# Block 7's rows of v summed by TensorE per token, alternating with block 6's rows summed by VectorE

## The chip, the cores and the metric

The kernel runs on one core of a Trainium2 chip. The metric is the device time of one execution in microseconds (us), as the median over runs. Engines are named as the profile names them: PE is TensorE (PEld its weight loads), DVE is VectorE, ACT is ScalarE, POOL is GpSimd, SP is SyncE. All compute engines work through their instructions in a fixed order that was set when the program was built.

## The reference

One layer over 1024 tokens of width 1024: a mixing part (RWKV-7 and latent attention, gated and added to x), then PEER, then a per-layer embedding and a last RMSNorm. The change lies in PEER, a retrieval over 16384 single-neuron experts. For each token 8 heads choose 16 experts each by product keys, so 128 expert numbers `idx` and 128 gates per token:

```python
act = jax.nn.gelu(jnp.einsum('td,thkd->thk', xb, u_tab[idx]), approximate=False)
return jnp.einsum('thk,thkd->td', gate * act, v_tab[idx])
```

`xb` is the normed x of a block of 128 tokens; `u_tab` and `v_tab` are tables of 16384 rows of 1024 f32 numbers. What is added to x is, for each token, a sum of 128 rows of `v_tab`, each times its own weight. After PEER comes `x + sigmoid(RMSNorm(x) @ W_pg) * (p @ W_ple)` and the final norm.

## The kernel before, in words

The 1024 tokens are eight blocks of 128, in four slices of two blocks for the mixing part. `everything` (L1064) lists the stages with a priority each; a scheduler builds from it the fixed order of each engine's instructions: of those that it takes to be ready, the smaller number goes first. So stages interleave. A tile in a pool has a tag and a number of buffers; a new tile of the same tag waits until the oldest buffer's last reader is done.

The weights of a block's experts are made by `gather` (L891): for each k of 128, POOL issues an indirect DMA (L900) that brings to partition t the row of u that token t has chosen as its k-th, and DVE multiplies it with h and sums it up (L902). After gelu the result goes into `gate`, 128 tokens by 128 choices.

The rows of v are summed in two ways. Blocks 0 to 4 go through `dense` (L968, priority 50): `expand` has written for each of them a matrix of weights, mostly zeros, over all 16384 experts, and `dense` multiplies it with the whole table v, read once. Of each piece of v (`vr`, 128x512) ACT makes a rounded part `vhi` (L280) and DVE the rest `vlo` (L282); PE then does three matmuls for each of the five blocks (L996 to L998), and after each eight pieces DVE adds the five accumulators to x (L1001). The five accumulators fill five banks of PSUM.

Blocks 5, 6 and 7 go through `add_rows` (L908, priorities 56, 57 and 58). For each k POOL gathers into a buffer, for all 128 tokens at once, the k-th row of v (L915, 512 KB), and DVE does x = x + row * gate[:, k] (L917). x of blocks 5 and 6 lies in the pool `xp`; x of block 7 takes the buffer `gh`, in which `gather` had its h, so the profile calls it gh. `row` (L882) hands out the buffers of the rows: a ring of seven (three tags of 3, 1 and 3 buffers), used by `gather` and `add_rows` alike. A gather into a buffer can be issued when the row that was in it has been used.

Last comes `ple` (L1019, priority 60) for the blocks in turn: `begin` squares and norms x, transposes it by PE in eight steps, with ACT and DVE splitting each into two parts; `end` does 60 matmuls, adds and norms, and writes the block out. It starts the `begin` of the next block before the `end` of a block. It can begin a block when that block's sum is complete.

Of the kernel before, what the change touches and what calls it, by code (L numbers as in the profile page):

```python
# [8 lines left out]
F = mybir.dt.float32  # L9
R = mybir.dt.float32r  # L10
I32 = mybir.dt.int32
# [3 lines left out]
OP = mybir.AluOpType  # L15
# [5 lines left out]
D = 1024  # L21
# [130 lines left out]
class Program:  # L152
# [752 lines left out]
            nc.vector.tensor_tensor(gate, gate, dots, op=OP.mult)  # L905


    def add_rows(self, b):  # L908
        nc = self.nc
        idx, gate = self.idx[b], self.gate[b]  # L910
        x = self.tile(*((self.gp, [128, D], F, "gh", 1) if b == 7 else (self.xp, [128, D], F, f"x{b}", 1)))
        nc.sync.dma_start(x, self.x1[b])
        for k in range(128):
            v = self.row()
            nc.gpsimd.indirect_dma_start(out=v[:], out_offset=None, in_=self.I["v"],  # L915
                                         in_offset=bass.IndirectOffsetOnAxis(ap=idx[:, k:k + 1], axis=0))
            nc.vector.scalar_tensor_tensor(x, v, gate[:, k:k + 1], x, op0=OP.mult, op1=OP.add)  # L917
        self.final[b] = x


    def expand(self, blocks, side="right"):
# [142 lines left out]
    def everything(self):  # L1064
        nc = self.nc
        order = [
            (0, self.project_rwkv, 0), (0.1, self.rwkv, 0), (0.2, self.project_rest, 0), (1, self.attend, 0),
            (1.5, self.select, 0), (50, self.gather, [0, 1]), (2, self.project_rwkv, 1), 
            (4.9, self.rwkv, 1), (5, self.project_rest, 1), (5.2, self.project_rwkv, 2), (5.5, self.attend, 1), (6, self.select, 1),
            (50, self.gather, [2, 3]),  # L1070
            (11.1, self.rwkv, 2), (10, self.project_rest, 2), 
            (11.2, self.project_rwkv, 3), (10.5, self.attend, 2), (11, self.select, 2), (51, self.gather, [4]),
            (49, self.expand, [0]), (16.1, self.rwkv, 3), (15, self.project_rest, 3), (49.5, self.attend, 3), (52.5, self.select, 3),
            (52, self.gather, [5]), (49, self.expand, [1, 2, 3, 4]), (60, self.ple_weights, 0), (53, self.more_rows, None),
            (53, self.gather, [6, 7]), (50, self.dense, 0),
            (56, self.add_rows, 5), (57, self.add_rows, 6), (58, self.add_rows, 7),
            (59, self.ple_weights, 1), (60, self.ple, range(8)),
        ]
        with ExitStack() as st:
            self.kp = self.pool(self.ctx, "cx", "right")  # L1080
            self.wp = self.pool(st, "wts", "left")
            begun = {}
            self.tc.cur_priority = PHASE // 20
            self.rope_tables()
            for prio, f, a in order:
                if f == self.more_rows:
                    st.close()
                    self.xp = self.pool(self.ctx, "dx", "left")
                    self.gp2 = self.pool(self.ctx, "rows", "left")
                    continue  # L1090
                self.tc.cur_priority = int(prio * PHASE)
                self.aux = nc.gpsimd if f == self.rwkv else nc.vector
                if f == self.project_rwkv:
                    begun[a] = f(a)
                elif f == self.attend:
                    f(a)
                    if a + 1 in begun:
                        begun[a + 1][1].close()
                elif f == self.project_rest:
                    begun[a][1].close()  # L1100
                    f(a, begun[a])
                elif f == self.ple_weights:
                    f(a, ("right", "left")[a])
                else:
                    f(a)
# [15 lines left out]
```

## Time and profile before

| | us |
|---|---|
| runs | 3947.78, 3949.66, 3959.03 |
| median of the runs | 3949.66 |
| the profiled execution's own time | 3942.72 |
| its span, first to last instruction | 3940.7 |
| PE busy | 3087.6 (78%) |
| DVE busy | 3193.8 (81%) |
| ACT busy | 1276.9 (32%) |
| POOL busy | 2050.4 (52%) |

The page gives each engine's busy time over the whole span. The stages differ, so the shares over the span say little about one of them; the views by stretch, further down, do that. Matmuls overlap in the engine, so PE's mean time of one matmul is longer than the distance from one to the next.

### The profile page before, as it was taken

What the parts mean: (1) busy time and instruction counts of PE and PEld (TensorE: products, weight loads), DVE (VectorE), ACT (ScalarE), POOL (GpSimd) and SP (SyncE); (2) the same over time, 40 slices, a digit from 0 to 9 for tenths busy, and PEclk for the clock granted to TensorE, in tenths of its full rate; (3) what the DMA queues carried; (4) which work ended last, traced back from release to release, by engine and by line L of the source; (5) the groups of instructions that cost most, each with busy time, mean ns of one, the idle gap of its engine ahead of it and who ended that gap; (6) DMA issues with size and microseconds to landing.
All of it is one profiled execution on the core that took longest, in us unless ns stands there. A gap on an engine that the chain in (4) does not pass through costs nothing.

```text
span 3940.7 us, 62191 instructions
## 1 busy us (share of the span) xinstructions
PE 3087.6 (78%) x21999; PEld 2517.8 (64%) x21999; DVE 3193.8 (81%) x6931; ACT 1276.9 (32%) x2723; POOL 2050.4 (52%) x1638
## 2 busy tenths in 40 slices
PE   7998778678879794878866687568888889989581
PEld 7885767666668673578735567446666667767351
DVE  2532888767899685899878778998999999999997
ACT  3231222133222174222138867522221222222341
POOL 0201456645654533576454425446767776666754
PEclk9998899888989796888967788779999999999796
DMA  6236598899868998878888998799999999999986
GB/s 200 88 112 200 183 321 286 285 318 309 313 188 309 322 323 285 305 243 279 311 276 284 302 336 274 233 321 341 386 384 371 390 379 372 373 385 352 329 279 232
DMA packets 502327, 1160.48 MB, mean 294 GB/s; under 512 B 54016, under 2 KB 228352, under 8 KB 502016
## 3 DMA queue, kind: packets, MB, share of 16 engines
q0 software_dynamic: 202752, 738.29, 52.7%
q1 hardware_dynamic: 281984, 402.48, 30.3%
q10 hardware_dynamic: 17280, 15.74, 1.2%
q8 instruction: 174, 2.85, 0.3%
q14 instruction: 137, 1.12, 0.1%
HBM read 1071.38 MB, written 84.93 MB: 293 GB/s over the span
## 4 chain that ended last, share of the span: by engine, by line
DVE 23%; PE 23%; issue 20%; DMA 17%; POOL 10%; ACT 5%; SPq 2%; POOLq 0%; DVEq 0%; ACTq 0%
DVE u L902 9%; DMA u<-in_u_dram,idx 9%; PE mm L290 7%; POOL u L900 6%; POOL u L915 4%; PE mm L785 2%; DVE oa L959 2%; PE w L961 1%; PE inv L586 1%; PE acc L997 1%; DMA u<-in_v_dram,idx 1%; DMA raw<-zT 1%; PE acc L998 1%; PE mm L292 1%; SPq L964 1%
## 5 line engine op out<-in xcount | busy, mean ns | idle before, releaser
L900 POOL DMA_INDIRECT u<-in_u_dram,idx x1024 | 1230.5, 1202 | 1182.1 <-DVE dots L902 625.2
L902 DVE CUSTOM_DVE_ANT_0 u<-u,gh 128x1024 f32<-128x1024 f32 x1024 | 1320.8, 1303 | 226.8 <-DMA u<-in_u_dram,idx 210.1
L915 POOL DMA_INDIRECT u<-in_v_dram,idx x384 | 485.7, 1265 | 230.6 <-DVE x L917 104.1
L290 PE MATMUL mm<-hT,w 128*128 128x128 f32 x4608 | 568.4, 284 | 11.8 <-DMA raw<-zT 3.5
L997 PE MATMUL acc<-vlo,Whi 128*128 128x512 f32 x1280 | 521.8, 408 | 67.4 <-DVE vlo L282 66.8
L290 PEld LDWEIGHTS mm<-hT,w 128*128 128x128 f32 x4608 | 553.1, 199 | 27.6 <-ACT z L326 7.8
L998 PE MATMUL acc<-vhi,Wlo 128*128 128x512 f32 x1280 | 513.4, 401 | 0.0
L996 PE MATMUL acc<-vhi,Whi 128*128 128x512 f32 x1280 | 374.3, 402 | 101.8 <-ACT vhi L280 83.0
L996 PEld LDWEIGHTS acc<-vhi,Whi 128*128 128x128 f32 x1280 | 244.9, 193 | 176.5 <-ACT vhi L280 93.1
L997 PEld LDWEIGHTS acc<-vlo,Whi 128*128 128x128 f32 x1280 | 248.4, 194 | 147.1 <-DVE vlo L282 96.7
L917 DVE SCALAR_TENSOR_TENSOR x<-u,gate,x 128x1024 f32<-128x1024 f32 x256 | 329.2, 1286 | 6.0 <-DMA u<-in_v_dram,idx 2.1
L280 ACT ACTIVATE vhi<-vr 128x512 fp32r<-128x512 f32 x256 | 158.8, 628 | 532.2 <-DMA vr<-in_v_dram 347.6
L961 PE MATMUL w<-ob,oa 128*128 128x128 f32 x1280 | 225.3, 334 | 98.1 <-ACT ob L955 53.5
L961 PEld LDWEIGHTS w<-ob,oa 128*128 128x128 f32 x1280 | 203.6, 240 | 124.9 <-ACT ob L955 81.6
L998 PEld LDWEIGHTS acc<-vhi,Wlo 128*128 128x128 f32 x1280 | 249.1, 195 | 51.6
L959 DVE TENSOR_SCALAR oa<-cst,pt 128x128 f32<-128x128 f32 x640 | 210.7, 388 | 39.3 <-PE w L961 34.8
L954 ACT ACTIVATE ob<-cst,pt 128x128 f32<-128x128 f32 x640 | 204.3, 396 | 0.6 <-PE w L961 0.5
L282 DVE TENSOR_TENSOR vlo<-vr,vhi 128x512 fp32r<-128x512 f32 x256 | 174.7, 693 | 8.0 <-ACT vhi L280 7.9
L280 ACT ACTIVATE Whi<-wr 128x1280 fp32r<-128x1280 f32 x64 | 81.5, 1273 | 287.0 <-PE acc L997 257.6
L917 DVE SCALAR_TENSOR_TENSOR gh<-u,gate,gh 128x1024 f32<-128x1024 f32 x128 | 167.9, 1311 | 4.9 <-DMA u<-in_v_dram,idx 3.0
L290 PE MATMUL mm<-act,w 128*128 128x256 f32 x512 | 134.0, 417 | 45.2 <-DMA act<-yg 29.1
L621 POOL TENSOR_TENSOR lm<-gs,cst 128x256 f32<-128x256 f32 x96 | 100.1, 1063 | 100.9 <-DVE gs L612 56.6
(331 smaller groups left out, 5511.6 us busy)
## 6 DMA issues: line engine op xcount, KB each, us to landing
w<-in_w_in_dram SPq DMA_DIRECT2D x144, 512.0 KB
vr<-in_v_dram SPq DMA_DIRECT2D x256, 256.0 KB
W<-ws SPq DMA_DIRECT2D x40, 1024.0 KB
wr<-W SPq DMA_DIRECT2D x64, 640.0 KB
w<-in_w_q_dram SPq DMA_DIRECT2D x64, 512.0 KB
w<-in_w_out_dram SPq DMA_DIRECT2D x32, 512.0 KB
u<-in_u_dram,idx POOLq DMA_INDIRECT x1024, 6.9
x<-in_x_dram SPq DMA_DIRECT2D x16, 512.0 KB
```

The lines of the kernel that those rows point to most:

```text
L280: self.nc.scalar.activation(act[0], x, AF.Copy)
L290: mm(ps, w[0][:, i], a[0][:, i], start=first, stop=last)
L900: nc.gpsimd.indirect_dma_start(out=u[:], out_offset=None, in_=self.I["u"], in_offset=bass.IndirectOffsetOnAxis(ap=idx[:, k:k + 1], axis=0))
L902: nc.vector.tensor_tensor_reduce(out=u[:], in0=u[:], in1=h[:], scale=1.0, scalar=0.0, op0=OP.mult, op1=OP.add, accum_out=dots[:, k:k + 1])
L915: nc.gpsimd.indirect_dma_start(out=v[:], out_offset=None, in_=self.I["v"], in_offset=bass.IndirectOffsetOnAxis(ap=idx[:, k:k + 1], axis=0))
L917: nc.vector.scalar_tensor_tensor(x, v, gate[:, k:k + 1], x, op0=OP.mult, op1=OP.add)
L954: nc.scalar.activation(c[:, i], self.c("iota"), AF.Abs, bias=pt[:, 1, k + i:k + i + 1])
L959: nc.vector.tensor_scalar(a, self.c("iota"), pt[:, 0, k:k + 1], pt[:, 2, k:k + 1], op0=OP.is_equal, op1=OP.mult)
L961: nc.tensor.matmul(ps[:, i], a, c[:, i], start=True, stop=True)
L996: nc.tensor.matmul(acc[b], wh, vh, start=i == 0, stop=False)
L997: nc.tensor.matmul(acc[b], wh, vl, start=False, stop=False)
L998: nc.tensor.matmul(acc[b], wl, vh, start=False, stop=i == G - 1)
```

## The change

`add_rows` takes a list of blocks. Block 5 is summed as before. Blocks 6 and 7 are one call, at priority 57: after every four rows of block 6, one step of the generator `sum_rows` runs for block 7. It gathers per token instead of per choice: `idx` and `gate` are transposed by PE, so that one gather brings to the 128 partitions the 128 chosen rows of one token. A matmul with weights of 128 rows by 32 columns, of which only the token's own column is not zero (it holds the token's 128 gates), adds the token's sum to its own row of PSUM and zeros to 31 others. Four tokens, 32j + i for j = 0 to 3, have their 32 columns side by side and write to the four quarters of the same two banks (one for each half of the 1024 columns); over the 32 steps i all 128 tokens are summed. DVE prepares the weights for four steps at a time, and at the end adds the two banks to x.

```diff
--- before.py
+++ after.py
@@ -905,17 +905,67 @@
             nc.vector.tensor_tensor(gate, gate, dots, op=OP.mult)
 
 
-    def add_rows(self, b):
-        nc = self.nc
-        idx, gate = self.idx[b], self.gate[b]
+    def rows_of_v(self, idx, k):
+        v = self.row()
+        self.nc.gpsimd.indirect_dma_start(out=v[:], out_offset=None, in_=self.I["v"],
+                                          in_offset=bass.IndirectOffsetOnAxis(ap=idx[:, k:k + 1], axis=0))
+        return v
+    def before_rows(self, b):
         x = self.tile(*((self.gp, [128, D], F, "gh", 1) if b == 7 else (self.xp, [128, D], F, f"x{b}", 1)))
-        nc.sync.dma_start(x, self.x1[b])
+        self.nc.sync.dma_start(x, self.x1[b])
+        self.final[b] = x
+        return x
+    def add_rows(self, blocks):
+        nc = self.nc
+        x = self.before_rows(blocks[0])
+        idx, gate = self.idx[blocks[0]], self.gate[blocks[0]]
+        tokens = self.sum_rows(blocks[1]) if len(blocks) > 1 else None
         for k in range(128):
-            v = self.row()
-            nc.gpsimd.indirect_dma_start(out=v[:], out_offset=None, in_=self.I["v"],
-                                         in_offset=bass.IndirectOffsetOnAxis(ap=idx[:, k:k + 1], axis=0))
+            v = self.rows_of_v(idx, k)
             nc.vector.scalar_tensor_tensor(x, v, gate[:, k:k + 1], x, op0=OP.mult, op1=OP.add)
-        self.final[b] = x
+            if tokens and k % 4 == 3:
+                next(tokens)
+        if tokens:
+            next(tokens)
+    def sum_rows(self, b):
+        nc = self.nc
+        x = self.before_rows(b)
+        fi = self.tile(self.gp, [128, 128], F, "dots", 1)
+        nc.vector.tensor_copy(fi, self.idx[b])
+        with ExitStack() as st:
+            psum = self.pool(st, "vp", "right", True)
+            acc = [self.tile(psum, [128, 512], F, f"sum{n}", 1) for n in range(2)]
+            nc.tensor.transpose(acc[0][:, 0:128], fi, self.ident)
+            nc.tensor.transpose(acc[0][:, 128:256], self.gate[b], self.ident)
+            idx = self.tile(self.sel, [128, 128], I32, "idx0", 1)
+            gate = self.tile(self.sel, [128, 128], F, "gate0", 1)
+            nc.vector.tensor_copy(idx, acc[0][:, 0:128])
+            nc.vector.tensor_copy(gate, acc[0][:, 128:256])
+            of = gate.rearrange("p (j i) -> p i j", j=4)
+            for i in range(32):
+                if i % 4 == 0:
+                    w = self.tile(self.kp, [128, 512], F, ("ts", "ti")[i // 4 % 2], 1)
+                    nc.vector.memset(w, 0.0)
+                    nc.vector.tensor_copy(w[:, i:i + 387].rearrange("p (i n) -> p i n", n=129)[:, :, 0:97:32], of[:, i:i + 3])
+                    nc.vector.tensor_copy(w[:, i + 387:i + 387 + 97:32], of[:, i + 3])
+                rows = [self.rows_of_v(idx, 32 * j + i) for j in range(4)]
+                for n in range(2):
+                    for j, v in enumerate(rows):
+                        o = i % 4 * 128 + 32 * j
+                        nc.tensor.matmul(acc[n][32 * j:32 * j + 32], w[:, o:o + 32], v[:, n * 512:n * 512 + 512],
+                                         start=i == 0, stop=i == 31)
+                yield
+            for n in range(2):
+                xd = x[:, n * 512:n * 512 + 512]
+                nc.vector.tensor_tensor(xd, xd, acc[n], op=OP.add)
+        yield
 
 
     def expand(self, blocks, side="right"):
@@ -1073,7 +1123,7 @@
             (49, self.expand, [0]), (16.1, self.rwkv, 3), (15, self.project_rest, 3), (49.5, self.attend, 3), (52.5, self.select, 3),
             (52, self.gather, [5]), (49, self.expand, [1, 2, 3, 4]), (60, self.ple_weights, 0), (53, self.more_rows, None),
             (53, self.gather, [6, 7]), (50, self.dense, 0),
-            (56, self.add_rows, 5), (57, self.add_rows, 6), (58, self.add_rows, 7),
+            (56, self.add_rows, [5]), (57, self.add_rows, [6, 7]),
             (59, self.ple_weights, 1), (60, self.ple, range(8)),
         ]
         with ExitStack() as st:
```

## Rows read from the trace of the kernel before

**Rows 1.** Page, costliest groups: operation, shapes, count | busy us, mean ns | idle before.

```profile
L917 DVE SCALAR_TENSOR_TENSOR x<-u,gate,x 128x1024 f32<-128x1024 f32 x256 | 329.2, 1286 | 6.0 <-DMA u<-in_v_dram,idx 2.1
...
L917 DVE SCALAR_TENSOR_TENSOR gh<-u,gate,gh 128x1024 f32<-128x1024 f32 x128 | 167.9, 1311 | 4.9 <-DMA u<-in_v_dram,idx 3.0
```

**Rows 2.** Busy time by stretch; columns named in the first line, clock and DMA as shares.

```profile
core 0: us, PE busy (x) PEld busy (x) DVE busy (x) ACT busy (x) POOL busy (x), PEclk, DMA share, GB/s
...
3421.00:3660.00 239.00, 209.58 (x879) 165.13 (x877) 229.47 (x241) 54.26 (x80) 162.09 (x125) 0.98 0.98 366
3660.00:3840.00 180.00, 126.90 (x486) 91.79 (x487) 167.92 (x264) 65.70 (x139) 123.33 (x97) 0.81 0.87 299
3840.00:3905.00 65.00, 1.28 (x6) 0.71 (x4) 60.63 (x50) 0.06 (x1) 45.01 (x41) 0.55 0.94 346
3905.00:3941.00 36.00, 17.86 (x68) 13.34 (x68) 12.20 (x32) 11.72 (x22) 0.00 (x0) 0.74 0.07 29
```

**Rows 3.** The same stretches, the gathers of rows of v alone (L915).

```profile
core 0: us, POOL busy (x), PEclk, DMA share, GB/s
...
3421.00:3660.00 239.00, 160.32 (x124) 0.98 0.98 366
3660.00:3840.00 180.00, 116.24 (x92) 0.81 0.87 299
3840.00:3905.00 65.00, 45.01 (x41) 0.55 0.94 346
```

**Rows 4.** Groups by line and shape, 3421 to 3660 us.

```profile
L915 POOL DMA_INDIRECT u<-in_v_dram,idx x124 | 160.6, 1295 | 75.4 <-DVE x L917 47.4 <-issue 24.4 <-DVE x L1001 1.2
L917 DVE SCALAR_TENSOR_TENSOR x<-u,gate,x 128x1024 f32<-128x1024 f32 x125 | 160.1, 1281 | 2.4 <-DMA u<-in_v_dram,idx 0.4
...
L282 DVE TENSOR_TENSOR vlo<-vr,vhi 128x512 fp32r<-128x512 f32 x57 | 38.8, 684 | 2.5 <-ACT vhi L280 2.4
L280 ACT ACTIVATE vhi<-vr 128x512 fp32r<-128x512 f32 x57 | 35.4, 629 | 125.3 <-DMA vr<-in_v_dram 70.6 <-PE acc L998 37.2 <-DVE x L917 16.0
```

**Rows 5.** DMA issues, gathers of v, median us to landing; 3421:3660, 3660:3840, 3840:3905.

```profile
u<-in_v_dram,idx POOLq DMA_INDIRECT x124, 7.6
...
u<-in_v_dram,idx POOLq DMA_INDIRECT x92, 5.9
...
u<-in_v_dram,idx POOLq DMA_INDIRECT x41, 5.9
```

**Rows 6.** POOL in order of time, 3848 to 3862 us: start, us, instruction [idle before].

```profile
3849.43 1.01 POOL L915 DMA_INDIRECT u<-in_v_dram,idx  x1 [0.30 <-issue]
3850.75 1.02 POOL L915 DMA_INDIRECT u<-in_v_dram,idx  x1 [0.30 <-issue]
3852.08 1.02 POOL L915 DMA_INDIRECT u<-in_v_dram,idx  x1 [0.30 <-issue]
```

**Rows 7.** Line 785 (f32, 512 columns), 345 to 352 us: count, durations, first and last start.

```profile
L785 PE MATMUL mm<-w,act x15: 592/592/592, 344.8 to 351.6; 128*128 128x512 f32 x15
...
L785 PE MATMUL tr<-w,act x2: 592/592/592, 348.6 to 349.1; 128*128 128x512 f32 x2
```

**Rows 8.** PE in order of time, 284.5 to 286.5 us: the column pair of attention.

```profile
284.87 0.65 PE L720 MATMUL acc<-pT,V 128*64 128x256 f32 x4
285.45 0.44 PE L714 MATMUL pt<-cst,pr 128*128 128x128 f32 x2
```

**Rows 9.** Line 917 over the span; the last gathers on POOL; DVE's last rows and last work.

```profile
L917 DVE SCALAR_TENSOR_TENSOR x<-u,gate,x x256: 1264/1280/2766, 3183.2 to 3676.9; 128x1024 f32<-128x1024 f32 x128
...
3899.24 1.31 POOL L915 DMA_INDIRECT u<-in_v_dram,idx  x1 [0.30 <-issue]
...
3901.37 5.25 DVE L917 SCALAR_TENSOR_TENSOR gh<-u,gate,gh 128x1024 f32<-128x1024 f32 x4 [0.32 <-DMA u<-in_v_dram,idx]
...
3935.82 1.28 DVE L1055 SCALAR_TENSOR_TENSOR gh<-gh,frsy,gf 128x1024 f32<-128x1024 f32 x1
```

More of the change, by code (lines that the diff above doesn't have):

```diff
@@ L905, in gather @@
             nc.vector.tensor_tensor(gate, gate, dots, op=OP.mult)
-    def add_rows(self, b):
+    def rows_of_v(self, idx, k):
[4 more added lines that the diff above has]
+    def before_rows(self, b):
+        x = self.tile(*((self.gp, [128, D], F, "gh", 1) if b == 7 else (self.xp, [128, D], F, f"x{b}", 1)))
+        self.nc.sync.dma_start(x, self.x1[b])
+        self.final[b] = x
+        return x
@@ L909, in add_rows @@
+    def add_rows(self, blocks):
         nc = self.nc
-        idx, gate = self.idx[b], self.gate[b]
-        x = self.tile(*((self.gp, [128, D], F, "gh", 1) if b == 7 else (self.xp, [128, D], F, f"x{b}", 1)))
-        nc.sync.dma_start(x, self.x1[b])
+        x = self.before_rows(blocks[0])
+        idx, gate = self.idx[blocks[0]], self.gate[blocks[0]]
+        tokens = self.sum_rows(blocks[1]) if len(blocks) > 1 else None
         for k in range(128):
-            v = self.row()
-            nc.gpsimd.indirect_dma_start(out=v[:], out_offset=None, in_=self.I["v"],
-                                         in_offset=bass.IndirectOffsetOnAxis(ap=idx[:, k:k + 1], axis=0))
+            v = self.rows_of_v(idx, k)
```

## The prediction

> **What bounds the kernel now.** I read the page first, then a table of stretches, then the stretch that the change touches by line, by landing time and in order of time. The page [rows 1] shows that the gathered rows of v are worth 128 DVE instructions of about 1.3 us for each of blocks 5, 6 and 7: 329.2 us for blocks 5 and 6 and 167.9 us for block 7. The reader should see in the stretches [rows 2] three stages. From 3421 to 3660 us `dense` runs beside block 6's rows: DVE is busy 229.5 of 239 us (96%), but the DMA engines are at 0.98 too, and PE has 239 - 209.6 = 29 us idle. From 3660 to 3840 us the per-block tail `ple` runs beside block 7's rows: DVE is 93% busy, DMA 0.87. From 3840 to 3905 us rows stand nearly alone.
>
> The 124, 92 and 41 gathers of the three stages [rows 3] make 256 (one lies across 3840), so block 6 begins with the first of them, at 3420.7 us. The pace is 239/124 = 1.93 us a row, then 180/92 = 1.96; with nothing else on DVE it is 1.32 [rows 6]. In the first stage POOL's waits are for DVE [rows 4]: a gather waits until the row seven before it in the ring of seven buffers is used. So DVE bounds the rows, but beside `dense` it isn't alone: the loads of `dense` are late because of DMA (70.6 us of ACT's idle time there ends with a landing of `vr`). Taking work from DVE can raise the pace mainly after 3660, where the 41 rows show that 1.32 is possible.
>
> **The change, part by part.** Removed: 128 DVE instructions, 167.9 us [rows 1]. Added to DVE: eight memsets and sixteen copies of 128x512 or less, three 128x128 copies, two additions out of PSUM. The 128x512 subtraction takes 0.684 us [rows 4], so at most 29 x 0.69 = 20 us, and no less than 0; beside 168 removed they need no place of their own, and only the last two additions (1.4 us) lie on the end's path. Moved: the load of block 7's x1, one DMA on SP whose buffer and source are long ready; its data are needed at the very end, so nothing. POOL issues the same 256 gathers, now four of block 6 and four of block 7 in turn. Before the first gather of block 7 stand two copies and two transposes, once; POOL and the rows behind it wait for these. Between 0 and a landing, 7.6 us [rows 5]; I take nothing, because four rows of block 6 are ahead of it.
>
> Added to PE: 256 matmuls of 128 rows by 32 columns, 512 moving f32 columns each. An f32 matmul stands as two records, and with 512 columns they start 6.8/16 = 0.425 us apart (17 from 344.8 to 351.6, [rows 7]), so 0.85 us for one by itself. No row shows four side by side. The nearest is the pair in attention [rows 8]: 4 records of 128x64 weights and 256 columns, after which the next group starts 0.58 us later. One after another they would need 4 x 0.2125 = 0.85 (half of 0.425 for half the columns); side by side 0.425 plus 0.155 for weights and the change of shape. So a group of four tokens costs, for both halves of the columns, 2 x (0.85 + 0.155) = 2.0 us; bounds are 1.7 (no overhead) and 6.8 (8 x 0.85, all in turn). I take 2.0, from the pair. 32 groups are 64 us.
> By the Trainium skill, page "TensorEngine Tiling (Array Packing)", section "Key Properties", a change of tiling mode drains TensorE, which speaks against mixing these groups into `dense`; the 0.155 us behind the pair holds such a change, so the row bears it out but makes it small. The page "TensorE: Matmul & The Clock Gate", Part 3, gives 2.38 times for three column tiles, not three; by that ratio a group would take 8 x 0.85/(4 x 0.79) = 2.1 us, an estimate from that page.
>
> **The new wait.** Four rows of block 7 are used together: the matmuls of the second half come after those of the first, which need all four rows. So all four buffers come free only when the last of the four has landed and PE is through. Then POOL must issue five gathers in order (one of block 6, four of block 7) before the next four can be complete. With R the moment of release, the fourth is issued 0.3 + 4 x 1.32 us after R [rows 6], lands 5.9 us after its start [rows 5], and PE takes 2.0: 0.3 + 5.3 + 5.9 + 2.0 = 13.5 us for 8 rows, 1.69 us a row. In the stretch with rows alone the clock was 0.55 of full, near the lower level of 1.2 GHz [rows 2]; there the group takes 4.0 and a row 15.5/8 = 1.94 us. Beside `dense` an issue takes 1.295 + 0.3 and a landing 7.6 us [rows 4, 5]: 0.3 + 6.4 + 7.6 + 2.0 = 16.3, or 2.04 us a row; between 1.90 (issue every 1.32) and 2.2 (PE has 1.5 us of `dense` ahead of the group). So the ring takes DVE's place as the bound, at much the same pace.
>
> **The sum.** Beside `dense`, 239/2.04 = 117 rows instead of 124. The DMA time that they leave could bring `dense` to an end earlier, but 117/8 = 15 groups are 29 us on PE, just its idle time; I leave the end at 3660. Then 139 rows remain, 60% of them with `ple` beside them (1.69) and 40% alone (1.94): 139 x 1.79 = 249 us, so the last gather is issued at 3909 instead of 3899 (the last start in [rows 9]). It lands 5.9 later, PE takes 2 to 4 and the two additions 1.4: block 7 is complete at 3919, not 3907 (3901.37 + 5.25, [rows 9]). What follows took 34 us. Now block 6 is complete only some 8 us before block 7, where its last addition began at 3677 before [rows 9]; its own `ple` shares PE and DVE with block 7's: 0 to 15 us more, as one block's 60 matmuls are about 14 us at the pace of `dense` (879 in 209.6 us, 0.24 each, [rows 2]). Most fits into block 7's chain of small steps, so I take 5. The end is 3919 + 39 = 3958, against a span of 3940.7: +17. The profiled execution took 3942.72, 7 us under the median of the runs (3949.66), so on the runs' scale 3949.66 + 17, rounded to 3966.
>
> **Rivals.**
> First, the ring doesn't hold (the rows keep the pace of the DMA engines): if the fixed order of the gathers lets later ones go before a blocked one, or landings come sooner, the rows run at about 1.38 us after 3660: the 41 last rows moved 346 GB/s at 0.94. That is the other side. For it speaks that only DVE was at its limit there; against it the four buffers held together. It decides from a loop under 12 us for 8 rows. 133 rows x 1.38 = 184 us instead of 239 is -55, the tail's +5 and block 7's later completion +3 leave -47: 3903.
> Second, PE waits inside `dense`: PE works in a fixed order, and each of 15 groups stands ahead of matmuls of `dense`. If it is reached before its rows have landed, `dense` stands still for up to 7.6 us. At half of that, 15 x 3.8 = 57 us; some 20 of it come back as rows get further ahead. With the forecast's +17 in part: 3990 to 4005. For it: PE has only 29 us of slack. Against: in the kernel before, DVE waits 0.4 us for rows in the same stretch [rows 4], though it had the same mixed order.
> Third, the change doesn't do what it says: four column groups run in turn. A group is then 6.8 us, a loop 13.5 + 4.8 = 18.3 (2.3 us a row), PE has 218 us more work, and the end moves by (2.3 - 1.8) x 139 = 70 us or more: 4035. The pair speaks against it.
>
> **How the numbers follow.** About 0.3% (12 us) is what a measurement of this kernel can tell from no change. The forecast's mechanism (the ring holds) has 0.56; its terms run from 1.69 us a row throughout after `dense` and no longer tail (-2: 3947; some 10 less with an issue of 1.25 us) to 1.94 throughout (+40: 3990; 10 more with the tail's 15), so within it faster is 0.08, same 0.19, slower 0.29. The first rival has 0.24 (faster 0.22, same 0.02), the second 0.15 (same 0.03, slower 0.12), the third 0.05. Together faster 0.30, same 0.24, slower 0.46. The range reaches to 3910 for most of the first rival and to 4005 for the second. Within the forecast's own case it is 3940 to 3995.
>
> **What would show it.** Right: POOL's idle time before gathers ends with PE instead of DVE; 8 rows take 13 to 16 us after `dense`; DVE has a quarter of its time free there; DMA stays under 0.9; PE's new groups take 2.0 us at full clock. Wrong: `dense` ends after 3680 us with PE idle until rows land (second rival); rows after `dense` come every 1.4 us (first); a group takes over 6 us (third). If block 6's `ple` costs over 15 us after block 7 is complete, the tail was sized wrongly.

## The result, and the profile after

The changed kernel takes 4009.82 us (median of 4 runs) against 3948.72 us for the kernel before: a ratio of 1.0143, with a 95% interval of 1.0116 to 1.0171. It is slower by 1.4%: some 57 us by the ratio, 61 by the medians alone; the forecast was 3966. The profiled execution took 4020.34 us (span 4018.5), the slowest of the four.

The last and first starts of two lines cut the span into parts. First the kernel before (source views of the gathers of v and of `dense`; durations are ns, min/median/max, then first and last start in us):

```profile
L915 POOL DMA_INDIRECT u<-in_v_dram,idx x384: 932/1126/2547, 3174.0 to 3899.2; - x192
...
L997 PE MATMUL acc<-vlo,Whi x1280: 387/389/796, 2590.3 to 3650.7; 128*128 128x512 f32 x183
```

The same two views of the kernel after:

```profile
L910 POOL DMA_INDIRECT u<-in_v_dram,idx x384: 932/1012/2547, 3188.9 to 3967.0; - x192
...
L1047 PE MATMUL acc<-vlo,Whi x1280: 387/389/796, 2601.8 to 3681.0; 128*128 128x512 f32 x183
```

The first gather of v, after which the kernels differ most, stands 15 us later in this execution, and `dense` began 11.5 us later, before any new instruction of weight. Nothing ties that to the change: four executions of the changed kernel lie between 3998 and 4020, and in the profiles of the nine kernels of this document with seven row buffers the first gather of v stands anywhere from 3168 to 3193. Counted from the first gather, the rest takes 4018.5 - 3188.9 = 829.6 instead of 766.7 us: 63 more, about what the medians say. Of these, 52.9 lie between the first and the last gather (778.1 instead of 725.2) and 10 after it (51.5 instead of 41.5).

The stretches, with the columns of [rows 2], show where the 53 are. From 3440 to 3681 `dense` runs beside the rows of blocks 6 and 7:

```profile
3440.00:3681.00 241.00, 237.28 (x1051) 170.42 (x1050) 146.46 (x170) 48.51 (x68) 111.96 (x99) 1.00 0.85 307
3681.00:3840.00 159.00, 141.53 (x515) 70.46 (x514) 89.08 (x181) 54.84 (x115) 94.13 (x81) 0.92 0.82 279
3840.00:3967.00 127.00, 80.73 (x238) 29.62 (x236) 63.95 (x68) 7.91 (x16) 83.94 (x82) 0.84 0.93 341
3967.00:4018.00 51.00, 37.27 (x154) 25.47 (x154) 22.66 (x60) 21.01 (x42) 1.02 (x1) 0.91 0.16 64
```

The reader should set the first line beside [rows 2]. DVE fell from 96% to 61%, as the change means it to. PE rose from 209.6 of 239 to 237.3 of 241 us: it has nothing left. POOL issued 99 gathers in 241 us (2.43 us each) where it issued 124 in 239 (1.93, [rows 3]), and the DMA engines fell from 0.98 to 0.85. So 25 fewer rows were issued in the same time, and at the pace after `dense` (286 us for 156, 1.83) they cost about 46 us. By parts, the 53 us are these: from block 6's first gather to the end of `dense` 11 more (241 instead of 230), from there to the last gather 38 more (286 instead of 248, for 156 rows instead of 134), and 4 in block 5's rows, which take 241 to 252 us in the profiles of all kernels here. The bound beside `dense` has moved from DVE to PE.

That PE isn't held up from outside there is shown by its waits in that stretch (us in total, times, longest), which come to 3.6 of 241 us:

```profile
PE acc L1047 <- DVE vlo L282: 1.9, 1, 1.9
PE acc L1046 <- DVE x L1051: 1.7, 1, 1.7
```

The groups of the same stretch answer to [rows 4]; POOL's idle time before a gather has grown from 75 to 126 us, and a good part of it now ends with the new matmuls (`sum`, L962); DVE, which had waited 0.4 us for rows, waits 46 us:

```profile
L910 POOL DMA_INDIRECT u<-in_v_dram,idx x99 | 112.0, 1131 | 125.9 <-DVE x L931 58.5 <-PE sum L962 35.8 <-issue 21.9
...
L931 DVE SCALAR_TENSOR_TENSOR x<-u,gate,x 128x1024 f32<-128x1024 f32 x57 | 73.0, 1280 | 51.5 <-DMA u<-in_v_dram,idx 46.3 <-issue 4.9
```

Last, the price of the new matmuls. PE's busy time under L962 in the two stretches before and after 3681 (the two leading numbers after the window are its length and PE's busy time, then the count):

```profile
3440.00:3681.00 241.00, 33.89 (x170) 7.17 (x170) 1.00 0.85 307
3681.00:3967.00 286.00, 124.93 (x326) 28.56 (x326) 0.89 0.87 307
```

A group of four tokens is 16 records, so it takes 33.89 x 16/170 = 3.2 us beside `dense` and 124.93 x 16/326 = 6.1 after it, not 2.0. PE in order of time shows why; the first line stands beside `dense`, the others among the matmuls of `ple`:

```profile
3548.70 1.91 PE L962 MATMUL sum<-u,ti 128*32 128x512 f32 x10
...
3823.92 1.92 PE L962 MATMUL sum<-u,ts 128*32 128x512 f32 x8
...
3836.93 1.90 PE L962 MATMUL sum<-u,ti 128*32 128x512 f32 x4
3838.77 0.33 PE L252 MATMUL tr<-cst,h 128*128 128x128 f32 x1
3839.03 1.90 PE L962 MATMUL sum<-u,ti 128*32 128x512 f32 x4
```

Ten records, eight and four all take 1.9 us. Four records are both halves of one token, and they stand one behind the other; eight are two tokens side by side. So the price goes by how often PE turns to the new matmuls, and not by how many tokens it then takes. Counted from PE in order of time, with a turn ending where a matmul of another line follows, it turns to them 17 times beside `dense` for 170 records, only five times with a whole group of 16; after `dense`, up to 3865 us, 31 times, 19 of them with one token, eight with two and never with four. In the fixed order a token's matmuls come where the scheduler took its row to be there, between those of other stages, so only where rows are taken to land together do tokens share the array. That the scheduler's guess of the landings makes the groups is read off this order; no run tests it by itself.

### The profile page after: what moved, and what is told of

It reads as the page before. It is cut to its first block, busy times and chain, and to the rows that moved or that the text cites. A ratio compares the mean times of both kernels' runs of the same rounds, so it can differ in the third digit from the quotient of the medians.

```text
span 4018.5 us, 62968 instructions
## 1 busy us (share of the span) xinstructions
PE 3246.8 (81%) x22513; PEld 2558.8 (64%) x22513; DVE 3052.6 (76%) x6832; ACT 1276.9 (32%) x2723; POOL 2031.0 (51%) x1638
## 4 chain that ended last, share of the span: by engine, by line
PE 30%; DVE 25%; DMA 17%; issue 15%; POOL 7%; ACT 4%; SPq 2%; POOLq 0%; DVEq 0%; another core or an unknown queue 0%; ACTq 0%
DVE u L902 10%; DMA u<-in_u_dram,idx 9%; PE mm L290 8%; POOL u L900 5%; PE acc L1047 2%; PE acc L1048 2%; PE mm L785 2%; PE acc L1046 2%; DVE x L931 2%; DVE oa L1009 2%; DMA u<-in_v_dram,idx 2%; PE sum L962 2%; POOL u L910 2%; PE w L1011 1%; PE inv L586 1%
## 5 line engine op out<-in xcount | busy, mean ns | idle before, releaser
L900 POOL DMA_INDIRECT u<-in_u_dram,idx x1024 | 1254.9, 1226 | 1176.3 <-DVE dots L902 593.0
L910 POOL DMA_INDIRECT u<-in_v_dram,idx x384 | 444.8, 1158 | 326.4 <-DVE x L931 125.7
L1046 PE MATMUL acc<-vhi,Whi 128*128 128x512 f32 x1280 | 392.8, 403 | 87.7 <-ACT vhi L280 62.6
L290 PEld LDWEIGHTS mm<-act,w 128*128 128x128 f32 x512 | 105.7, 213 | 67.0 <-issue 29.9
```

The source lines that it names most:

```text
L290: mm(ps, w[0][:, i], a[0][:, i], start=first, stop=last)
L900: nc.gpsimd.indirect_dma_start(out=u[:], out_offset=None, in_=self.I["u"], in_offset=bass.IndirectOffsetOnAxis(ap=idx[:, k:k + 1], axis=0))
L910: self.nc.gpsimd.indirect_dma_start(out=v[:], out_offset=None, in_=self.I["v"], in_offset=bass.IndirectOffsetOnAxis(ap=idx[:, k:k + 1], ax ...
L1046: nc.tensor.matmul(acc[b], wh, vh, start=i == 0, stop=False)
```

## The experiments

Two theories were put to the test. **PE**: the new matmuls cost PE 3 to 6 us for four tokens, and PE is full beside `dense`. **Ring** (also called buffers): the rows are late because seven buffers are held, by four at a time or by a fixed order, whatever PE takes. The table has the ratios to the kernel before, the pace of the gathers in us a row (window length by count, profiled execution) from block 6's first gather to the end of `dense` and from there to the last gather, and PE's whole busy time under the new matmuls in us. The kernel before stands at 1.90 here and at 1.93 in [rows 3] because `dense` ends at 3651 there and the stretch at 3660.

| run | ratio | 95% interval | beside dense | after dense | PE, new matmuls |
|---|---|---|---|---|---|
| before | 1 | | 230/121 = 1.90 | 248/134 = 1.85 | |
| after | 1.0143 | 1.0116 to 1.0171 | 241/99 = 2.43 | 286/156 = 1.83 | 165 |
| e1_half | 1.0056 | 1.0036 to 1.0076 | 239/115 = 2.08 | 244/141 = 1.73 | 112 |
| e2_single | 1.0020 | 1.0007 to 1.0033 | 235/114 = 2.06 | 241/143 = 1.69 | 77 |
| e3_together | 1.0302 | 1.0269 to 1.0334 | 226/70 = 3.23 | 359/186 = 1.93 | 128 |
| e4_late | 1.0190 | 1.0169 to 1.0211 | 229/120 = 1.91 | 320/135 = 2.37 | 190 |
| e5_late_single | 1.0004 | 0.9985 to 1.0022 | 231/120 = 1.93 | 248/135 = 1.84 | 91 |
| e6_ring8 | 1.0191 | 1.0149 to 1.0232 | 372/177 = 2.10 | 164/79 = 2.08 | 162 |
| e7_single_ring8 | 1.0027 | 1.0011 to 1.0044 | 327/184 = 1.78 | 132/72 = 1.83 | 61 |
| e8_before_ring8 | 0.9970 | 0.9951 to 0.9988 | 292/163 = 1.79 | 182/94 = 1.94 | |
| e9_together_single | 1.0137 | 1.0107 to 1.0168 | 217/88 = 2.47 | 297/168 = 1.77 | 34 |
| e10_before_trims | 0.9995 | 0.9979 to 1.0011 | 231/121 = 1.91 | 246/136 = 1.81 | |

**Half of the new matmuls.**

```diff
-                for n in range(2):
+                for n in range(1):
                     for j, v in enumerate(rows):
...
-            for n in range(2):
+            for n in range(1):
                 xd = x[:, n * 512:n * 512 + 512]
```

> Block 7's second 512 columns are left out: half of the new matmuls, everything else as in the changed kernel (256 gathers, same ring). Theory PE: the new matmuls run one token at a time and take 3 to 6 us of PE for four tokens instead of 2.0, and PE has only 29 us beside dense; half the work should bring the pace of the rows beside dense from 2.43 to about 2.0 us and end near 3965 us (3950 to 3980). Theory ring: the rows are late because four buffers are held together and used in a fixed order, PE time is of no weight; the end stays within 15 us of 4010.

Measured 3974.09 us, within the range of theory PE. The pace beside `dense` went from 2.43 to 2.08 and the loss fell from 1.43% to 0.56%, as theory PE has it; with the ring untouched, theory ring falls for this part. Half of the matmuls are not half of PE's time: over the whole run the new ones take 112 us instead of 165, a third less. The gathers by stretch (POOL's busy time with the count), then the new matmuls (PE's busy time with the count first):

```profile
3438.00:3677.00 239.00, 129.65 (x115) 1.00 0.92 340
3677.00:3921.00 244.00, 154.06 (x141) 0.87 0.92 328
...
3438.00:3677.00 239.00, 27.35 (x104) 3.74 (x104) 1.00 0.92 340
3677.00:3921.00 244.00, 79.58 (x144) 10.04 (x144) 0.87 0.92 328
```

**One pass instead of two records.**

```diff
-                        nc.tensor.matmul(acc[n][32 * j:32 * j + 32], w[:, o:o + 32], v[:, n * 512:n * 512 + 512],
+                        nc.tensor.matmul(acc[n][32 * j:32 * j + 32], high(w[:, o:o + 32]), high(v[:, n * 512:n * 512 + 512]),
```

with `high` the upper 16 bits of each f32 number, read as bf16: the kernel leaves out the lower halves of block 7's rows and gates.

> The new matmuls read only the upper halves of the f32 numbers (as bf16), so each is one pass of 512 columns (about 0.23 us) instead of two records of 0.43: a quarter of the PE time, values of v and gates cut to bf16 for block 7. Theory PE: the loss goes away, 3930 to 3960 us, and PE is under 95% beside dense. Theory ring: no change beyond 15 us from 4010.

Measured 3960.58 us, 0.2% slower than before. So about six sevenths of the loss (1.43 - 0.20 of 1.43) go when PE's time under the new matmuls falls from 165 to 77 us. The time itself is just above the expected 3930 to 3960, and PE didn't come under 95% beside `dense` as was expected: it is at 97%, and 20 us of that are the new matmuls (the last two lines):

```profile
3438.00:3673.00 235.00, 229.11 (x987) 168.29 (x985) 152.86 (x177) 48.36 (x68) 130.90 (x114) 0.99 0.93 343
3673.00:3914.00 241.00, 158.03 (x568) 82.46 (x567) 147.83 (x241) 62.86 (x131) 162.63 (x149) 0.76 0.93 335
...
3438.00:3673.00 235.00, 19.69 (x104) 3.73 (x104) 0.99 0.93 343
3673.00:3914.00 241.00, 52.89 (x144) 6.99 (x145) 0.76 0.93 335
```

The paces left, 2.06 and 1.69, are those that the prediction's loop gave (2.04 and 1.69), but by chance: the loop was worked out for four buffers held together, and here they come free token by token.

**Four tokens together.**

```diff
                 for n in range(2):
-                    for j, v in enumerate(rows):
+                    for j in (3, 0, 1, 2):
...
+                        if n or j < 3:
+                            self.tc.keep_in_program_order(m)
```

> The eight matmuls of four tokens are kept in program order behind the one of the token gathered last, so that they are ready at once and can run side by side; all else as in the changed kernel. Theory PE: the new matmuls take 2.0 to 2.5 us of PE for four tokens, and the end comes to what the prediction's sum gave, 3955 to 3985 us. Theory ring: buffers are held longer than in the changed kernel, where a token's buffer comes free after its own two matmuls; 4020 to 4060 us.

Measured 4063.56 us, 3.0% slower than before: the worst of all, a little beyond what theory ring expected. Where the group stands together it does take what the pair of columns had promised, 16 records in 1.92 us (PE in order of time, with the matmuls before and behind):

```profile
3591.53 0.39 PE L1050 MATMUL acc<-vhi,Wlo 128*128 128x512 f32 x1
3591.85 1.92 PE L962 MATMUL sum<-u,ti 128*32 128x512 f32 x16
3593.70 0.50 PE L1048 MATMUL acc<-vhi,Whi 128*128 128x512 f32 x1
```

It seldom stands together whole. The matmul of the token gathered last goes first and mostly alone, two records in some 1.0 us, so that a group took 20.74 x 16/112 = 3.0 us beside `dense` and 103.64 x 16/384 = 4.3 after it, at a granted clock of 0.74, and not the 2.0 to 2.5 that theory PE expected:

```profile
3424.00:3650.00 226.00, 20.74 (x112) 3.79 (x112) 0.99 0.73 258
3650.00:4009.00 359.00, 103.64 (x384) 17.22 (x384) 0.74 0.82 287
```

Still PE spent less on the new matmuls than in the changed kernel (128 us instead of 165), and the kernel is slower. The price of holding four buffers until the group's place in PE's order comes is far higher than the loop said: beside `dense` 70 rows in 226 us. POOL's waits from 3424 to 3650 (us in total, times, longest) show single waits of up to 22.7 us for the group, and nearly twice as many us in all for rows of block 6, whose own gathers stand behind those of the group in the same ring; in the changed kernel the longest of either are 6.9 and 6.7 us:

```profile
POOL u L910 <- DVE x L931: 66.7, 21, 8.6
POOL u L910 <- PE sum L962: 35.4, 7, 22.7
```

**Four together, in one pass.** The edits of e2_single and e3_together at once.

> The third experiment's order (four tokens' matmuls together, all four buffers held until the last has landed) with the one-pass matmuls of the second. The changed kernel lost 61 us and the grouped one about 115. If what the grouping adds is PE time in another shape, one pass takes it away: 3955 to 3975 us, as the second experiment. If it is the hold of four buffers and the place of a whole group behind dense's matmuls, it stays: 4010 to 4050 us.

Measured 4002.87 us, 1.4% slower than before: 7 us under the range for the hold, far above the one for PE time. The four kernels make a square: one by one 1.0143 and 1.0020, together 1.0302 and 1.0137 (f32 and one pass). Each of the two, PE's time and the hold of four, costs 1.2 to 1.7% whichever way the other stands; the step to one pass took about as much from PE each time (165 to 77 us, 128 to 34). So the hold is real, and it isn't PE time in another shape. In the changed kernel itself the hold isn't paid, since the tokens go one by one, and PE's time is paid for it.

**Block 7 by TensorE after dense.**

```diff
-            (56, self.add_rows, [5]), (57, self.add_rows, [6, 7]),
+            (56, self.add_rows, [5]), (57, self.add_rows, [6]), (58, self.add_rows, [7]),
...
+        if blocks == [7]:
+            for _ in self.sum_rows(7):
+                pass
+            return
```

> Block 6 is summed by VectorE alone as in the kernel before, then block 7 alone by TensorE, so that the new matmuls come after dense. Theory PE: dense ends as in the kernel before (about 3651), and after it PE has ple's 127 us and 128 tokens at 1.5 to 1.7 us one by one, some 320 to 345 us in all: 4010 to 4050 us. Theory ring (PE time of no weight): without VectorE's share the rows run near the pace of issue, 1.4 to 1.6 us, and the end is 3900 to 3930 us, faster than the kernel before.

Measured 4023.38 us, within the range of theory PE. `dense` now ends as before, but after it PE is at 94%; the stretch of all engines, and the new matmuls alone:

```profile
3644.00:3964.00 320.00, 300.73 (x983) 118.72 (x981) 91.12 (x221) 72.35 (x151) 144.28 (x141) 0.98 0.74 244
...
3644.00:3964.00 320.00, 181.71 (x488) 37.56 (x488) 0.98 0.74 244
```

488 records in 181.7 us are 6.0 us for 16, and 2.37 us a row. So the loss isn't only that `dense` is in the way: one token at a time, PE is too slow for rows beside `ple` as well.

**Late and in one pass.** The edits of e2_single and e4_late at once.

> Both edits at once: block 7 by TensorE after block 6 (so after dense), and the matmuls as one pass over the upper halves (block 7's rows and gates cut to bf16). Theory PE: with 128 tokens at under 0.7 us of PE after dense, neither PE nor VectorE holds the rows; they come at the pace of issue and landing, 1.35 to 1.5 us, for about 136 rows after 3650: end near 3890 (3880 to 3915), faster than the kernel before. Theory buffers: seven buffers and the fixed order hold the rows at 1.7 us or more whatever PE takes: 3930 to 3950.

Measured 3947.56 us, no different from the kernel before (0.9985 to 1.0022): theory PE's 3890 fails, and the time lies in theory buffers' range of 3930 to 3950. With neither DVE nor PE full (90 and 204 of 248 us busy), the rows still came every 1.84 us. PE in order of time shows what holds a landed row:

```profile
3756.81 0.62 PE L967 MATMUL sum<-u,ts 128*32 128x512 bf16 x2
3757.36 0.33 PE L252 MATMUL tr<-cst,h 128*128 128x128 f32 x1
3757.87 0.50 PE L292 MATMUL mm<-w_pp1hi,phi 128*128 128x512 f32 x1 [0.18 <-ACT sg L1103]
...
3762.10 0.63 PE L967 MATMUL sum<-u,ts 128*32 128x512 bf16 x2
```

Between two tokens stands `ple`'s own block of matmuls, 4.3 us, after a wait of 0.18 us for ACT; POOL, meanwhile, waits with the next gather:

```profile
3758.14 0.94 POOL L910 DMA_INDIRECT u<-in_v_dram,idx  x1 [0.30 <-issue]
3763.00 0.94 POOL L910 DMA_INDIRECT u<-in_v_dram,idx  x1 [3.92 <-PE tr L252]
```

The Trainium skill says of PE, in "TensorE: Matmul & The Clock Gate", Part 2, that matmuls stay in program order and only weight loads are pulled ahead; this trace agrees: the token's two matmuls start at 3762.10, behind all matmuls of that block.

The wait is no single case. From 3660 to 3900, POOL's two longest waits (us in total, times, longest) end with PE:

```profile
POOL u L910 <- PE sum L967: 56.6, 37, 4.7
...
POOL u L910 <- PE tr L252: 18.8, 17, 3.9
```

An issue by itself takes 0.94 + 0.30 us, so these 75 us are most of what lies between 1.24 and 1.84 us a row (0.6 x 135 = 81). PE waited for rows to land for 17.9 us in that time, so part of the hold is the landing. Which stands for how much wasn't separated: no run changes the order on PE alone.

**Eight row buffers**, in the changed kernel, with the one-pass matmuls, and in the kernel before; and the trims that make room for the eighth, alone.

```diff
-ROWS = (4, 7)
+ROWS = (4, 8)
...
-            pair = lambda k, tag: [t([128, k, 128], tag + x, HB, R) for x in ("hi", "lo")]
+            pair = lambda k, tag: [t([128, k, 128], tag + x, HB if k == 8 else 1, R) for x in ("hi", "lo")]
...
-                    sg = t([128, 512], "sg", 2)
+                    sg = t([128, 512], "sg", 1)
```

> The changed kernel with eight row buffers instead of seven; room is made in ple by one buffer instead of two for its sigmoid and for the split of p. Theory PE: beside dense PE is full already and the pace there stays at 2.4 us a row; 3998 to 4015. Theory buffers: one buffer more saves an issue, 1.3 us in each eight rows, 256 rows x 0.165 = 42 us at most: 3970 to 3985.

> Eight buffers with the one-pass matmuls of the second experiment. If what is left there (2.06 us a row beside dense, 1.69 after it) is the ring, the pace goes to about 1.9 and 1.5 and the end from 3960 to 3920 to 3940; if it is something else (landing, the fixed order of PE), it stays at 3950 to 3965.

> The kernel before with eight row buffers and the same two trims in ple: what the trims and the eighth buffer do without the change. VectorE bounds the rows there, so within 6 us of the kernel before (both theories); more than 10 us slower would be the trims, more than 10 faster would mean that the ring held the kernel before as well.

> The kernel before with the two trims in ple alone (one buffer for the sigmoid and for the split of p), seven row buffers: the control for the eighth buffer. If the 0.3% of the eighth experiment is the buffer, this is within 0.2% of the kernel before; if it is the trims, it is 0.3% faster as well.

Measured 4026.15, 3961.00, 3936.22 and 3947.22 us. In the changed kernel the eighth buffer gained nothing: 1.0191 is not below 1.0143, and 4026 lies above the ranges of both theories. With one pass it gained nothing either: 1.0027 after 1.0020, and 3961 lies in the range for "something else". Yet the ring had held the rows beside `dense`, where the pace went from 2.43 to 2.10 and from 2.06 to 1.78 us a row: the rows got ahead, and other work fell behind. With one pass `dense` ended at 3743 instead of 3673 us, the DMA engines at 1.00 beside it, and 89 us instead of 53 were left after the last gather. In the changed kernel with eight buffers `dense` lasted until 3781 us with PE at 98%, and 83 us were left after the last gather (columns of [rows 2]). The trims alone were run in the kernel before only, so what they cost in these two is open:

```profile
3409.00:3781.00 372.00, 364.36 (x1464) 228.55 (x1462) 219.84 (x249) 63.05 (x89) 203.23 (x177) 1.00 0.89 325
3781.00:3945.00 164.00, 132.49 (x463) 60.41 (x462) 86.98 (x156) 44.88 (x94) 96.22 (x85) 0.91 0.82 286
3945.00:4028.00 83.00, 68.04 (x293) 47.87 (x291) 37.96 (x106) 38.27 (x79) 0.94 (x1) 0.96 0.14 52
```

In the kernel before it is a gain: 0.9970, interval 0.9951 to 0.9988, where the trims alone give 0.9995 (0.9979 to 1.0011). That is the fastest kernel measured, by about 0.3%. It is 11 us by the medians, more than the 6 that were expected, and small enough to be named with its interval each time; the two intervals overlap a little, so that the gain is the buffer's and not the trims' is likely, not shown. Beside `dense` DVE is at 99% and the DMA engines at 1.00, and the rows of v come every 1.79 us instead of 1.90:

```profile
3412.00:3704.00 292.00, 254.93 (x1045) 197.14 (x1045) 288.42 (x290) 58.52 (x81) 205.44 (x163) 0.98 1.00 381
```

But the time isn't gained there. The first starts of the two lines that cut the span:

```profile
L997 PE MATMUL acc<-vlo,Whi x1280: 387/389/796, 2591.0 to 3703.5; 128*128 128x512 f32 x183
...
L915 POOL DMA_INDIRECT u<-in_v_dram,idx x384: 932/1097/2606, 3161.1 to 3885.4; - x192
```

From the first gather of v to the end this execution takes 3933.3 - 3161.1 = 772 us, against 767 in the kernel before. From the first start of L997 to that gather, while the ring serves the rows of u, it takes 570 us against 584; there the three kernels with eight buffers take 570 to 578 and the nine with seven 584 to 595, the trims alone 589. So by these profiles the eighth buffer pays in the rows of u, ahead of the stretch that this change is about.

## Why the prediction was right or wrong

The direction was right (slower), the size wrong: +17 us forecast, some 57 to 61 measured, outside the range of 3910 to 4005 by 5 us.

The step that failed is "a group of four tokens costs, for both halves of the columns, 2 x (0.85 + 0.155) = 2.0 us", and with it "32 groups are 64 us" and "15 groups are 29 us on PE, just its idle time". The price of a full group was right: 16 records take 1.92 us in e3_together. What was wrong is that most of the kernel's groups aren't full: beside `dense` five of PE's 17 turns have all 16 records. The diff's loop writes eight matmuls in a row, and the forecast read this as PE's order; the order is made by the scheduler, matmul by matmul. Measured, the group takes 3.2 us beside `dense` and 6.1 after it, 159 us in all before 3967 where 64 were forecast. The bounds of 1.7 and 6.8 held; the value taken between them was the wrong end, and the third rival, which had 6.8 as its mechanism, was given 0.05 because it was thought of as a question of the array alone.

From it follows the rest. "117 rows instead of 124" beside `dense` became 99, because PE was full with ten groups where 15 were to fit, and `dense` took 11 us longer from block 6's first gather to its end (3650.7 - 3420.7 = 230 before, 3681 - 3440 = 241 after). With the ring as it was, a third off the new PE time (165 to 112 us) gave back 0.9% of the 1.4, and half off (to 77 us) 1.2%: that PE's time is the cause is shown.

"All four buffers come free only when the last of the four has landed": not so in the changed kernel, for the same reason; there a token's buffer comes free after its own two matmuls. The loop that was worked out from it describes the kernels where four are held. After `dense` it does well: 1.93 us a row in e3_together and 1.77 in e9_together_single, within the forecast 1.69 to 1.94. Beside `dense` it gave 2.04, and the two took 3.23 and 2.47: the time that a complete group waits for its place among the matmuls of `dense` was put at 1.5 us at most, and in e3_together single waits reach 22.7. So a second step failed here: e3_together, the nearest to the kernel that the forecast had in mind, is 3.0% slower and not 0.4%.

The pace in "139 x 1.79" after `dense` came out at 1.83 (for 156 rows), and that is luck, as is the sign of 13 to 16 us for 8 rows (14.7): not the hold made it, and not a low clock. The granted clock was 0.92 and 0.84 in the two stretches there, where 40% of the rows had been put at 0.55; PE had the tokens one by one and was busy 141.5 of 159 and 80.7 of 127 us.

The tail was sized well: 49 us from the last gather to the end in the forecast (5.9 + 3 + 1.4 + 34 + 5), 51.5 measured, 41.5 before. Where block 6 is complete early, in e4_late, it is 4007.3 - 3964.0 = 43.3; so some 8 of the 10 us go with block 6's `ple`, which has no rows left to hide it.

The second rival (PE waits inside `dense`) is refuted for the changed kernel: `dense` did end after 3680, the sign that was named for it, but PE waited only 3.6 us there. The first (the rows go free, about 1.38 us a row) is refuted by every run that has the change, even where neither DVE nor PE was full: none is under 1.69 after `dense`. Its pace was also put too low: 524288 bytes at 346/0.94 = 368 GB/s are 1.42 us, by which its time would have been 3908.

## What to carry to other kernels

Work moved to an engine that seems to have room must be priced in the order in which that engine will meet it: matmuls that are cheap only side by side have to become ready together, and what makes them ready together (here four held buffers) has a price of its own (1.2 to 1.6% here). Before an engine's slack is spent, read the slack in the stretch where the work will land: PE had 29 us there, and the new work took 34 for ten of the fifteen groups that it was to carry. And where a ring of buffers is emptied by an engine with a fixed order, look at what stands ahead in that order, too: one token took PE 0.62 us in e5_late_single, and the rows still came every 1.84.

## What had not been expected of the hardware

In e3_together 16 records of four tokens side by side (each 128x32 weights, 512 columns, f32) stood in 1.92 us, where the 4 records of one token alone take 1.90 us in the changed kernel. From the start of either to the next matmul's start it is 1.85 us (3591.85 to 3593.70) and 1.84 (3836.93 to 3838.77): three more tokens for nothing measurable.

One pass takes a third of the time in f32, for one token and for several. A token alone is two records in 0.62 us (e5_late_single) against four in 1.90. Beside `dense` PE spent 19.69 us on 31 turns in e2_single, 0.64 each, against 33.89 on 17 in the changed kernel, 2.0 each. That a group of four still cost half as much there and not a third (19.69 x 8/104 = 1.5 us against 3.2) is the order again: 20 of the 31 turns took one token.
